# Gated attention in two streams, a softmax divided at the gates, and scan levels 2 and 4 in one group

## The chip, the cores and the metric

The kernel runs on one core of one Trainium2 chip. The metric is the time of one execution on the device in microseconds (us). Before the change it was run three times: 2367.55, 2368.6 and 2372.68 us, a median of 2368.6 us. One more execution was profiled, and all rows of the trace are from that one.

## The reference

Two layers over 2560 tokens (a prompt of 2048 and a sample of 512), 1024 wide. The even layer has two mixers side by side: A, a gated linear attention in both directions (4 heads of 128), and B, softmax attention in a window of 128 tokens to either side (8 query heads of 64 on 2 heads of keys and values). The odd layer is a gated short convolution. Cut to what the change touches:

```python
def swa_mixer(q, k, v, z, rel_bias, sink):
    ...
    s = jnp.einsum('bnqkgd,bnskd->bnkgqs', qh, kb).astype(jnp.float32) + bias
    s = jnp.where(mask, s, -jnp.inf)
    sk = sink.astype(jnp.float32).reshape(SWA_KV_HEADS, SWA_GROUP)[:, :, None, None]
    m = jnp.maximum(jnp.max(s, -1, keepdims=True), sk)
    e = jnp.exp(s - m)
    p = e / (jnp.sum(e, -1, keepdims=True) + jnp.exp(sk - m))
    o = jnp.einsum('bnkgqs,bnskd->bnqkgd', p.astype(v.dtype), vb).reshape(Bn, L, SWA_WIDTH)
    return o * jax.nn.silu(z)
```

In A, token j counts for token i with the weight q_i . (k_j x the product of the decays between them), the decays being numbers below one for each of the 128 channels. `o_f` runs over j <= i and `o_b` over j > i; their sum is normed and multiplied by silu(z).

## The kernel before

The tokens stand in 20 chunks of 128 (`c`) and 5 groups of 512 (`g`; group 4 is the sample, groups 0 to 3 the prompt). The work on TensorE is of two kinds.

*The dense stream* (`dense_ch`, `dense_tok`) are the projections, in a fixed order of stages (`run`, L2103): the input projection of groups 4, 3, 2 and 1, the output projection of group 4, the input projection of group 0, the odd layer of group 4, the output projection of group 0, and so on. A float32 product is made of three fast ones: each operand is split in a high part (`wh`, `st`) and a low one (`wl`). A unit of `dense_ch` (L569) has 16 matmuls of 128x512 on wh and 8 on wl, into one PSUM bank `acc`. ScalarE casts a raw weight tile `ws` to `wh`, GpSimd makes `wl` of the difference in four pieces (`cook`, `cook_low`, L531 to L556). SyncE's queue loads the raw tiles, and every other DMA of the kernel stands in that same queue.

*The side streams* are Python generators, whose pieces are put between the dense matmuls. `gla_stream` (L1454) takes the chunks of a group from the last to the first. For each it runs `inside` (L1186): the decayed products inside a chunk by doubling. At level s (1, 2, 4, ... 64), the queries in the tile Q ("QQ") and the keys in the tile K ("KK") hold the decays inside blocks of s tokens. One level is 16 matmuls of 32x32 (8 of 64x64 at the last), and VectorE grows Q and K to the next level between them. The keys of levels 2 to 16 are copied by ScalarE to a compact tile `km`. At level 8 the queries are copied aside too (`qm`, a tile "md"), and level 8 is computed together with level 16, in one visit to TensorE:

```python
            if s in (8,):
                qm = self.m2(hold=True)
                nc.scalar.copy(qm[:].rearrange("p (b two s) -> p b two s", two=2, s=s), halves(Q, s))
                wait.append((li, s, qm))
```

The same generator then does the chunk's part behind the levels: four transposes of K for each direction, the products with v, the state of the backward direction. Only then does it go on to the next chunk. `along` carries the forward state through the chunks at the end.

`swa_front` (L1510) computes the scores of B, their row maxima (VectorE), exponentials and sums (ScalarE), the reciprocals `den`, and multiplies the four tiles of P by them on VectorE (L1571). `swa_back` (L1579) transposes P on TensorE, splits it in `pth` and `ptl`, multiplies with V, and GpSimd multiplies the result `o` by the gate `gb` for each chunk (L1652).

*The order* is made when the program is built. `Model` (L97) keeps a clock for each engine by a cost for each operation, and when each tile is written and free. `Flow.pump` (L337) runs at each step of the dense stream. It takes the side streams by rank (0, 1, 2), then by the time at which what they wait for is ready, and lets one go on if its time has come and the clocks of VectorE and ScalarE stand less than about 4 us ahead. The scan has rank 1, `swa_front` and `swa_back` rank 2. A stream that says `yield x` waits for a time, for tiles, or for a mark. On the chip each engine runs its own queue in that order and waits on semaphores.

Of the kernel before, what the change touches and what calls it, by code (L numbers as in the profile page):

```python
# [262 lines left out]
class Flow:  # L263
# [32 lines left out]
    def flush(self, everything=False, name=None):  # L296
        now, keep = [], []
        for one in self.late:
            (now if everything or name in one[2] or (name is None and one[0] <= self.t) else keep).append(one)
        self.late = self.model.late = keep  # L300
        for one in now:
            one[1]()
# [74 lines left out]
class Trunk:  # L377
    def __init__(self, tc, nc, I, y_out, ctx):
        self.model = Model()
        self.nc = Engines(nc, self.model)  # L380
        self.tc, self.I, self.y_out = tc, I, y_out
        self.flow = Flow(self.model)
        P = lambda name, bufs, **k: ctx.enter_context(tc.tile_pool(name=name, bufs=bufs, **k))
        self.const = P("const", 1)
        self.stp = P("stp", 8)
        self.wp = P("wp", 2)
        self.yp = P("yp", 4)
        self.e2 = P("e2p", 1)
# [24 lines left out]
        self.bst = None  # L413
        self.blocks = []
# [154 lines left out]
    def dense_ch(self, xh, xl, w=None, last=True):  # L569
# [3 lines left out]
        p = self.pd()  # L573
# [13 lines left out]
        if last:  # L587
            self.drop(wl)
        return p
# [86 lines left out]
    def setup(self):  # L676
# [9 lines left out]
        self.dtot = c.tile([128, NC, 4], F32, name="dtot")  # L686
# [492 lines left out]

    def gla_load_k(self, c):  # L1180
        K = self.e((128, 2, 512), "KK")
        for i in range(2):
            self.nc.sync.dma_start(K[:, i], self.k_s[c])
        return K

    def inside(self, c, first, last, ld, K, ahead):  # L1186
# [3 lines left out]
        Q = self.e((128, 2, 512), "QQ")  # L1190
# [10 lines left out]

        acmp = self.sm((128, 4, 32), "acmp")
# [17 lines left out]
        def grow_k(s):  # L1220
# [12 lines left out]
        Sb = self.bst if not last else None  # L1233
        wait = []
        for li, s in enumerate((1, 2, 4, 8, 16, 32, 64)):
            n = 512 // s
            pls = []
            if s in (8,):
# [3 lines left out]
            else:  # L1242
# [14 lines left out]
                for lt, t, qm in wait:  # L1257
# [3 lines left out]
                    self.drop(qm)  # L1261
# [24 lines left out]
                kms.pop(s, None)  # L1286
# [14 lines left out]
            if s not in (8,):  # L1301
                grow_q()
# [5 lines left out]
            if s in (8,):  # L1308
                grow_q()
# [5 lines left out]
            if s == 4:  # L1315
                v = self.e((128, 512), "v")
                nc.sync.dma_start(v[:], self.v_s[c])
            yield [Q] if s < 16 else [Q, K]
        end = tots[128]
# [3 lines left out]
        nc.vector.tensor_copy(self.dtot[:, c], mk(end, 4, [[1, 4]]))  # L1323
        ahead(0)
        self.flow.defer(lambda: nc.sync.dma_start(self.qf_s[c], Q[:, 1]), Q)

        def turn(i):
# [3 lines left out]
            t = self.e((128, 4, 128), "km", bufs=2)  # L1331
# [3 lines left out]
        def grow(t):  # L1335
            pv = self.pw((128, 4, 128))
            for h in range(4):
                nc.tensor.matmul(pv[:, h], t[:, h], v[:, h * 128:h * 128 + 128], start=True, stop=True)
            return pv

        kf = kb = None
        if not last:
            yield from self.bank()
            kf = turn(0)
# [4 lines left out]
                                  acmp[:].unsqueeze(2).broadcast_to(wide))  # L1349
        if not first:  # L1350
            yield from self.bank()
            kb = turn(1)
        ahead(1)
# [10 lines left out]
        if not first:  # L1364
# [6 lines left out]
            else:  # L1371
                for h in range(4):
                    nc.vector.scalar_tensor_tensor(Sn[:, h], Sb[:, h], mk(end, h, [[1, 1]]), pv[:, h],
# [8 lines left out]
        yield [Q]  # L1382
# [19 lines left out]
    def along(self, c, first, last, ld, ahead):  # L1402
# [13 lines left out]
        if not last:  # L1416
# [4 lines left out]
            else:  # L1421
                for h in range(4):
                    nc.vector.scalar_tensor_tensor(Sn[:, h], Sf[:, h], self.dtot[:, c, h:h + 1], m[:, h],
# [29 lines left out]

    def gla_stream(self):  # L1454
        for g in (4, 3, 2, 1, 0):
# [3 lines left out]
            cs = list(range(4 * g + 3, 4 * g - 1, -1))  # L1459
            ld, K = self.gla_load(cs[0]), self.gla_load_k(cs[0])  # L1460
            nxt = {}
            for i, c in enumerate(cs):
                yield [*ld, K]

                def ahead(n):
                    if i < 3:
                        nxt[n] = (self.gla_load, self.gla_load_k)[n](cs[i + 1])
                yield from self.inside(c, *ends(c), ld, K, ahead)
                ld, K = nxt.get(0), nxt.get(1)
            if 4 * g > c0:  # L1470
                continue
            self.bst = None
            ld = K = None
            nxt.clear()
# [35 lines left out]
    def swa_front(self):  # L1510
# [7 lines left out]
        def best():  # L1518
# [4 lines left out]
            key = (lambda c: c) if "done_e1_0" in done else (lambda c: (-(c // 4), c))  # L1523
# [3 lines left out]
        while left:  # L1527
# [10 lines left out]
            for kv in range(2):  # L1538
# [3 lines left out]
                Pt = self.e((128, 4, 385), "P", bufs=4)  # L1542
# [36 lines left out]
    def swa_back(self):  # L1579
# [17 lines left out]
        for n in range(40):  # L1597
# [20 lines left out]
            for kb in range(nk):  # L1618
# [14 lines left out]
                yield []  # L1633
            yield [pl, V]
            Pt = None
# [15 lines left out]
            yield [gb]  # L1651
# [451 lines left out]
    def run(self):  # L2103
# [70 lines left out]
        flow.add(self.swa_front())  # L2174
        flow.add(self.swa_back())
# [29 lines left out]
```

## Time and profile before

| what | value |
|---|---|
| median of three runs | 2368.6 us (2367.55 to 2372.68) |
| the profiled execution | 2370.12 us |
| its span, first to last instruction | 2368.1 us |
| granted clock of TensorE | 0.998 |
| HBM read and written | 319.72 and 114.84 MB |
| share of the DMA engines by the kernel's own queue | 56.5% |

The span is what the trace shows; 2.0 us of the execution lie around it. An engine's busy time is the union of its instructions. The ends of matmuls are modelled and matmuls overlap each other, so the time that a row of TensorE gives is longer than its share; the step from one row's start to the next row's start is what it costs the queue. A float32 matmul of the scan leaves two records in the trace, a fast or a transposing one leaves one.

### The profile page before, as it was taken

To read this page: it belongs to the slowest core of one execution; us is meant where nothing else is said; L and a number is where in the kernel's file an instruction comes from. 1 tells how busy PE (TensorE), PEld (TensorE's weight loads), DVE (VectorE), ACT (ScalarE), POOL (GpSimd) and SP (SyncE) were. 2 spreads that over 40 slices of the span, in tenths; PEclk is the share of its full clock that TensorE was granted. 3 is DMA by queue.
4 is the path that set the end of the run, shared out by engine and by line. 5 is a ranking of instruction groups with operands and counts; after the bars stand their busy time and mean duration, and the time that the engine had idled before them with its cause. 6 is when DMAs were issued, how large, how long until landed. Compare 5 with 4: busy or idle time off the path is not lost.

```text
span 2368.1 us, 43087 instructions
## 1 busy us (share of the span) xinstructions
PE 2343.9 (99%) x15830; PEld 1951.8 (82%) x15830; DVE 1582.8 (67%) x2699; ACT 1226.1 (52%) x2363; POOL 1418.4 (60%) x1610
## 2 busy tenths in 40 slices
PE   8999999999999999999999999999999999999998
PEld 8888889888988888888888888878888877888887
DVE  2267756767767677577776467876566587656567
ACT  4666776656576645665577532543334343333431
POOL 5454435443444444444444467898887689988674
PEclk9999999999999999999999999999999999999999
DMA  7977686676667657675478777232124633221573
GB/s 230 295 226 233 221 269 229 209 221 221 218 194 236 223 173 242 197 218 161 158 245 268 266 261 243 92 116 89 52 78 140 217 105 103 73 72 58 175 242 121
DMA packets 275057, 437.37 MB, mean 185 GB/s; under 512 B 21360, under 2 KB 160240, under 8 KB 274848
## 3 DMA queue, kind: packets, MB, share of 16 engines
q1 hardware_dynamic: 274848, 434.64, 56.5%
q8 instruction: 125, 2.05, 0.4%
q14 instruction: 84, 0.69, 0.1%
HBM read 319.72 MB, written 114.84 MB: 184 GB/s over the span
## 4 chain that ended last, share of the span: by engine, by line
PE 87%; DVE 5%; POOL 4%; DMA 2%; issue 1%; ACT 1%; SPq 0%; POOLq 0%; DVEq 0%; ACTq 0%
PE acc L242 71%; PE ps L242 17%; POOL wl L242 1%; POOL wh L242 1%; DVE st L242 1%; DVE bst L242 1%; DVE y L242 1%; POOL md L242 0%; SPq L242 0%; DVE QQ L242 0%; DVE P L242 0%; DVE KK L242 0%; DMA K<-kb_s 0%; DMA mix_s<-gb 0%; DMA op_s<-QQ 0%
## 5 line engine op out<-in xcount | busy, mean ns | idle before, releaser
L242 POOL TENSOR_TENSOR wl<-ws,wh 128x256 fp32r<-128x256 f32 (+1 forms) x912 | 750.7, 855 | 711.4 <-PE acc L242 478.0
L242 PE MATMUL acc<-st,wh 128*128 128x512 f32 x3160 | 828.5, 395 | 2.8 <-DVE pr L242 2.0
L242 PEld LDWEIGHTS acc<-st,wh 128*128 128x128 f32 x3160 | 580.9, 188 | 121.0 <-issue 3.1
L242 PE MATMUL acc<-st,wl 128*128 128x512 f32 x1744 | 471.9, 395 | 2.8 <-POOL wl L242 1.9
L242 PE MATMUL acc<-wh,st 128*128 128x512 f32 (+1 forms) x1680 | 389.4, 371 | 7.9 <-ACT st L242 6.4
L242 PEld LDWEIGHTS acc<-st,wl 128*128 128x128 f32 x1744 | 320.8, 188 | 68.0 <-POOL wl L242 4.1
L242 PEld LDWEIGHTS acc<-wh,st 128*128 128x128 f32 x1680 | 300.2, 189 | 55.1 <-ACT st L242 6.4
L242 ACT CAST wh<-ws 128x1024 fp32r<-128x1024 f32 (+2 forms) x252 | 249.0, 989 | 184.2 <-DMA ws<-in_w_oo 55.9
L242 PE MATMUL acc<-wl,st 128*128 128x512 f32 (+1 forms) x840 | 209.0, 368 | 0.6 <-POOL wl L242 0.5
L242 ACT ACTIVATE md<-md 128x512 f32<-128x512 f32 x264 | 164.7, 631 | 20.5 <-DVE md L242 14.9
L242 PEld LDWEIGHTS acc<-wl,st 128*128 128x128 f32 x840 | 150.7, 188 | 23.8 <-POOL wl L242 1.3
L242 DVE SCALAR_TENSOR_TENSOR md<-acc,md 128x512 f32<-128x512 f32 (+1 forms) x113 | 77.0, 683 | 81.5 <-ACT md L242 76.5
L242 DVE TENSOR_TENSOR st<-pr,st 128x512 fp32r<-128x512 f32 x115 | 98.5, 874 | 41.6 <-ACT st L242 41.2
L242 ACT ACTIVATE md<-acc 128x512 f32<-128x512 f32 (+1 forms) x133 | 76.2, 597 | 67.0 <-PE acc L242 66.5
L242 POOL TENSOR_TENSOR wh<-md,wh 128x256 fp32r<-128x256 f32 x118 | 96.7, 842 | 13.6 <-ACT wh L242 13.1
L242 ACT CAST pth<-ps 128x512 fp32r<-128x512 f32 x112 | 65.3, 583 | 73.1 <-PE ps L242 72.3
L242 DVE CUSTOM_DVE_ANT_0 P<-ps,P 128x384 f32<-128x384 f32 (+1 forms) x160 | 79.3, 525 | 29.6 <-PE ps L242 29.0
L242 ACT ACTIVATE P<-P,nm 128x385 f32<-128x385 f32 (+1 forms) x160 | 93.2, 587 | 3.9 <-DVE nm L242 3.9
L242 ACT ACTIVATE mv<-mv,eps 128x1 f32<-128x1 f32 x40 | 11.8, 295 | 151.8 <-DVE mv L242 147.7
L242 PE MATMUL acc<-P,wh 128*128 128x512 f32 x312 | 89.5, 400 | 0.4 <-POOL wh L242 0.4
L242 ACT COPY km<-KK 128x512 f32<-128x512 f32 x80 | 50.8, 635 | 72.2 <-DVE KK L242 50.9
L242 ACT CAST st<-pr 128x512 fp32r<-128x512 f32 x115 | 68.3, 617 | 30.3 <-DMA pr<-mix_s 12.9
(490 smaller groups left out, 4090.2 us busy)
## 6 DMA issues: line engine op xcount, KB each, us to landing
ws<-in_w_ch SPq DMA_DIRECT2D x105, 512.0 KB, 4.4
ws<-in_w_od SPq DMA_DIRECT2D x58, 512.0 KB, 4.2
ws<-in_w_oe SPq DMA_DIRECT2D x40, 512.0 KB, 3.8
ws<-in_w_oo SPq DMA_DIRECT2D x36, 512.0 KB, 3.5
K<-kb_s SPq DMA_DIRECT2D x32, 384.0 KB, 6.3
d_s<-md SPq DMA_DIRECT2D x40, 256.0 KB, 4.2
qb_s<-md SPq DMA_DIRECT2D x80, 128.0 KB, 3.9
tA<-d_s SPq DMA_DIRECT2D x20, 512.0 KB, 5.7
```

The costliest lines, as they stand in the source:

```text
L242: r = f(*a, **k)
```

## The change

It has four parts.

1. *The scan becomes two streams.* What follows the levels moves from `inside` to `behind`, which `gla_behind` runs for each chunk as soon as its levels are done. K, Q and the totals of a chunk are handed over, so the levels of the next chunk can stand beside the rest of the last one. K and Q may now also lie in tiles "y" (`gla_home`), and the transposed K and the copies km in tiles "md". At most two chunks are under way (`self.open`).
2. *Level 2 is done with level 4.* The queries of level 2 are copied aside as those of level 8 are, and the two levels are computed in one visit.
3. *The softmax is divided at the gates.* P is no longer multiplied by the reciprocals. They are stored to `rd_s` as soon as they are there, for both heads of keys, and loaded late, each row spread over 64 partitions, into a tile "md" (`rb`). GpSimd multiplies the gate by them, then the result by the gate.
4. *Ranks and repairs.* `swa_front` and `swa_back` get rank 1, and `swa_front` chooses its chunks by another mark. `dense_ch` holds its bank while it uses it, and `flush` takes a deferred action off its list before it runs it.

```diff
@@ Trunk.__init__
+        self.rd_s = dr("rd_s", (NC, 2, 4, 128))
@@ dense_ch
-        p = self.pd()
+        p = self.pd(hold=True)
...
+        self.drop(p)
@@
+    def gla_home(self, tag):
+        done = self.flow.done
+        rows = "swa_in1" in done and "res_x1_4_3" not in done
+        return [(self.e2, tag, 1)] if rows or self.model.spare(tag, 1) else self.large[:1]
@@ inside
-        Q = self.e((128, 2, 512), "QQ")
+        while self.free_at(self.gla_home("QQ")) > self.flow.t:
+            yield 0.3
+        Q = self.take(self.gla_home("QQ"), (128, 2, 512))
...
+        while self.open > 1:
+            yield 0.3
+        self.open += 1
...
-                    km = kms[2 * s] = self.e((128, 512), "km", bufs=2)
+                    km = kms[2 * s] = self.take([(self.e2, "km", 2)] + self.mids, (128, 512))
...
-            if s in (8,):
+            if s in (2, 8,):
+                while self.free_at(self.mids) > self.flow.t:
+                    yield 0.3
                 qm = self.m2(hold=True)
...
-            if s not in (8,):
+            if s not in (2, 8,):
                 grow_q()
...
-        end = tots[128]
+        nc.vector.tensor_copy(self.dtot[:, c], mk(tots[128], 0, [[1, 8]]))
+        self.heads.append((c, first, last, K, Q, base, acmp))
+        self.flow.mark("head_%d" % c)
+
+    def behind(self, c, first, last, K, Q, base, acmp, v, ahead):
...
-            t = self.e((128, 4, 128), "km", bufs=2)
+            t = self.m2((128, 4, 128), hold=True)
@@
+    def gla_behind(self):
+        nxt = []
+        for c in [*range(19, 15, -1), *range(15, -1, -1)]:
+            yield "head_%d" % c
+            v = nxt.pop() if nxt else self.load_v(c)
...
+            yield from self.behind(*self.heads.pop(0), v, ahead)
@@ swa_front
-                for h in range(4):
-                    nc.vector.tensor_scalar(Pt[:, h, :w], Pt[:, h, :w], den[:, h:h + 1], None, op0=ALU.mult)
-                    if h == 1:
-                        yield []
+                def sums(c=c, kv=kv, den=den):
+                    nc.sync.dma_start(self.rd_s[c, kv].rearrange("h t -> t h"), den[:])
+                    if kv:
+                        self.flow.mark("rd_%d" % c, max(0.0, self.model.clock["sync"] - self.flow.t) + 10.0)
+                self.flow.defer(sums, den)
@@ swa_back
+            if kv:
+                yield "rd_%d" % c
+                while self.free_at(self.mids) > self.flow.t:
+                    yield 0.3
+                rb = self.m2(hold=True)
+                a = self.rd_s
+                for i in range(2):
+                    nc.sync.dma_start(rb[64 * i:64 * i + 64], bass.AP(a.tensor, a.offset + (2 * c + i) * 512, [[0, 64], [1, 512]]))
...
-            yield [gb]
+            yield [gb, rb]
+            flat = gb[:].rearrange("p h t -> p (h t)")
+            nc.gpsimd.tensor_tensor(flat, flat, rb[:], op=ALU.mult)
+            self.drop(rb)
+            yield [o]
             nc.gpsimd.tensor_tensor(gb[:], o[:], gb[:], op=ALU.mult)
@@ run
         flow.add(self.gla_stream(), rank=1)
-        flow.add(self.swa_front())
-        flow.add(self.swa_back())
+        flow.add(self.gla_behind(), rank=1)
+        flow.add(self.swa_front(), rank=1)
+        flow.add(self.swa_back(), rank=1)
```

How the order moves at two places. First TensorE's queue at the first chunk's levels 1 to 4, beside the input projection of group 3 (`acc<-st,wh` and `acc<-st,wl` are dense, `qn,KK` the diagonal, `QQ,KK` level 1, and `QQ,km` levels 2 and 4, each with one visit of its own). Before:

```order
L242 MATMUL acc<-st,wh 128x512 x14
L242 MATMUL ps<-qn,KK 32x32 x16
L242 MATMUL ps<-QQ,KK 32x32 x16
L242 MATMUL acc<-st,wh 128x512 x2
L242 MATMUL acc<-st,wl 128x512 x8
L242 MATMUL acc<-st,wh 128x512 x8
L242 MATMUL ps<-QQ,km 32x32 x16
L242 MATMUL acc<-st,wh 128x512 x8
L242 MATMUL acc<-st,wl 128x512 x8
L242 MATMUL ps<-QQ,km 32x32 x16
L242 MATMUL acc<-st,wh 128x512 x16
```

The same place of the changed kernel, where `md,km` is level 2 with its queries in a copy:

```order
L242 MATMUL ps<-qn,KK 32x32 x16
L242 MATMUL ps<-QQ,KK 32x32 x16
L242 MATMUL acc<-st,wh 128x512 x2
L242 MATMUL acc<-st,wl 128x512 x8
L242 MATMUL acc<-st,wh 128x512 x16
L242 MATMUL acc<-st,wl 128x512 x8
L242 MATMUL acc<-st,wh 128x512 x10
L242 MATMUL ps<-md,km 32x32 x16
L242 MATMUL ps<-QQ,km 32x32 x16
L242 MATMUL acc<-st,wh 128x512 x6
```

Level 2 has moved behind 26 more dense matmuls and stands next to level 4, which has itself moved behind 10 more. In all, TensorE has 13061 matmuls in either program.

Second, GpSimd's queue, where the gates of two chunks stand early in the attention among the low parts of the weights (`wl`). Before:

```order
L242 TENSOR_TENSOR wl<-y,wh 128x168 x4
L242 TENSOR_TENSOR wl<-ws,wh 128x256 x12
L242 TENSOR_TENSOR gb<-gb 128x512
L242 TENSOR_TENSOR wl<-ws,wh 128x256 x20
L242 TENSOR_TENSOR gb<-gb 128x512
```

At the gates of two chunks early in the changed kernel, where `gb<-gb,md` is the multiplication of the gate by the reciprocals:

```order
L242 TENSOR_TENSOR wl<-ws,wh 128x256 x20
L242 TENSOR_TENSOR gb<-gb,md 128x512
L242 TENSOR_TENSOR gb<-gb 128x512
L242 TENSOR_TENSOR wl<-ws,wh 128x256 x32
L242 TENSOR_TENSOR gb<-gb,md 128x512
L242 TENSOR_TENSOR wl<-ws,wh 128x256 x4
L242 TENSOR_TENSOR gb<-gb 128x512
```

A second multiplication has come in front of that of each gate, mostly right before it. On SyncE's queue 40 stores of `den` to `rd_s` and 40 loads of it come in (1304 DMAs before, 1386 after), and VectorE's queue has 160 instructions less.

More of the change, by code (lines that the diff above doesn't have):

```diff
@@ L296, in flush @@
     def flush(self, everything=False, name=None):
[L297 to L300, printed above, removed]
+        now = [one for one in self.late if everything or name in one[2] or (name is None and one[0] <= self.t)]
         for one in now:
-            one[1]()
+            if any(one is x for x in self.late):
+                self.late[:] = [x for x in self.late if x is not one]
+                one[1]()
     def force(self, *tiles):
@@ L1232, in inside @@
         base = None
-        Sb = self.bst if not last else None
         wait = []
@@ L1322, in inside @@
         self.drop(base)
-        nc.vector.tensor_copy(self.dtot[:, c], mk(end, 4, [[1, 4]]))
-        ahead(0)
+        base = None
         self.flow.defer(lambda: nc.sync.dma_start(self.qf_s[c], Q[:, 1]), Q)
@@ L1338, in grow, with place @@
                 nc.tensor.matmul(pv[:, h], t[:, h], v[:, h * 128:h * 128 + 128], start=True, stop=True)
+            self.drop(t)
             return pv
+        def place():
+            yield from self.bank()
+            while self.free_at(self.mids) > self.flow.t:
+                yield 0.3
         kf = kb = None
         if not last:
-            yield from self.bank()
+            yield from place()
             kf = turn(0)
@@ L1349, in inside @@
                                   acmp[:].unsqueeze(2).broadcast_to(wide))
+        self.open -= 1
         if not first:
-            yield from self.bank()
+            yield from place()
             kb = turn(1)
-        ahead(1)
+        self.drop(K)
         yield [A, v] + ([Sb] if Sb is not None else [])
@@ L1452, in seq, with ahead @@
         return (0, 16) if g < 4 else (16, 20)
+    def gla_behind(self):
[3 more added lines that the diff above has]
+            v = nxt.pop() if nxt else self.load_v(c)
+            def ahead():
+                if c not in (0, 16) and "gla_in%d" % ((c - 1) // 4) in self.flow.done:
+                    nxt.append(self.load_v(c - 1))
+            yield from self.behind(*self.heads.pop(0), v, ahead)
+            v = None
     def gla_stream(self):
+        nxt = {}
         for g in (4, 3, 2, 1, 0):
@@ L1458, in gla_stream, with ahead @@
             ends = lambda c: (c == c0, c == c1 - 1)
[L1459 to L1462, printed above, removed]
-                yield [*ld, K]
-                def ahead(n):
-                    if i < 3:
-                        nxt[n] = (self.gla_load, self.gla_load_k)[n](cs[i + 1])
+            for c in range(4 * g + 3, 4 * g - 1, -1):
+                if 0 not in nxt:
+                    nxt[0] = self.gla_load(c)
+                while 1 not in nxt:
+                    if self.free_at(self.gla_home("KK")) <= self.flow.t:
+                        nxt[1] = self.gla_load_k(c)
+                    else:
+                        yield 0.3
+                ld, K = nxt.pop(0), nxt.pop(1)
+                yield [*ld, K]
+                def ahead(s):
+                    if c > c0 and "gla_in%d" % ((c - 1) // 4) in self.flow.done:
+                        if s == 4:
+                            nxt[0] = self.gla_load(c - 1)
+                        elif self.free_at(self.gla_home("KK")) <= self.flow.t:
+                            nxt[1] = self.gla_load_k(c - 1)
                 yield from self.inside(c, *ends(c), ld, K, ahead)
-                ld, K = nxt.get(0), nxt.get(1)
+                ld = K = None
             if 4 * g > c0:
                 continue
+            yield "tail_%d" % c0
             self.bst = None
-            ld = K = None
-            nxt.clear()
             yield "done_e1_%d" % g
```

40 lines of the change are left out of this document (26 added, 14 removed).

## The prediction

> **What bounds the kernel now.** I read the page first: the span, the busy shares, the slices, the chain that ended last.
>
> ```profile
> span 2368.1 us, 43087 instructions
> PE 2343.9 (99%) x15830; PEld 1951.8 (82%) x15830; DVE 1582.8 (67%) x2699; ACT 1226.1 (52%) x2363; POOL 1418.4 (60%) x1610
> PEclk9999999999999999999999999999999999999999
> PE 87%; DVE 5%; POOL 4%; DMA 2%; issue 1%; ACT 1%; SPq 0%; POOLq 0%; DVEq 0%; ACTq 0%
> ```
>
> TensorE is busy for 99% of the span, at the full clock in every slice, and 87% of the chain is its own matmuls. The other engines are free for a third to a half of the time. So the question for every edit is: does it take a matmul, a step between matmuls, or a wait out of TensorE's queue, or put one in? Next I read the engines by stretch, and the waits of TensorE from 100 to 1400 us, where both attentions run beside the dense projections.
>
> ```profile
> 100.00:1250.00 1150.00, 1148.14 (x10441) 966.34 (x10440) 809.03 (x1711) 719.59 (x1474) 513.10 (x643) 1.00 0.68 217
> 1600.00:1800.00 200.00, 200.00 (x875) 163.95 (x874) 119.83 (x149) 75.08 (x108) 171.14 (x179) 1.00 0.23 78
> 1880.00:2368.00 488.00, 475.80 (x2104) 388.55 (x2102) 337.20 (x415) 183.07 (x292) 380.13 (x391) 1.00 0.36 123
> PE ps L242 <- ACT pth L242: 0.7, 1, 0.7
> PE acc L242 <- POOL wl L242: 0.5, 1, 0.5
> PE ps L242 <- DVE acmp L242: 0.2, 1, 0.2
> ```
>
> The columns of a stretch are its length, then busy us and instructions of PE, PEld, DVE, ACT and POOL. In the attention stretch TensorE lacks 1150 - 1148.14 = 1.9 us, and the longest single wait is 0.7 us. So **no wait is there to be won**: at most 1.9 us. The rest of the stretch can only get shorter if TensorE's own stream does. The stretch of 1600 to 1800 us, which has dense matmuls alone, gives the price of one: 200 us / 875 = 0.2286 us.
>
> **The change part by part.** *The matmuls* are the same in number and shape before and after, since the level of 2 is only put off and computed beside the level of 4. What changes is how often TensorE turns from the dense stream to a group of small matmuls and back. The timeline of TensorE at the first chunk shows what a turn costs (start, us, then name, shape and count; a 32x32 matmul of the program leaves two records):
>
> ```profile
> 118.67 3.33 PE L242 MATMUL acc<-st,wh 128*128 128x512 f32 x14
> 121.94 0.46 PE L242 MATMUL ps<-qn,KK 128*32 128x32 f32 x32
> 122.21 0.56 PE L242 MATMUL ps<-QQ,KK 128*32 128x32 f32 x32
> 122.70 0.73 PE L242 MATMUL acc<-st,wh 128*128 128x512 f32 x2
> 123.27 2.00 PE L242 MATMUL acc<-st,wl 128*128 128x512 f32 x8
> 125.10 1.98 PE L242 MATMUL acc<-st,wh 128*128 128x512 f32 x8
> 127.01 0.46 PE L242 MATMUL ps<-QQ,km 128*32 128x32 f32 x32
> 127.40 2.11 PE L242 MATMUL acc<-st,wh 128*128 128x512 f32 x8
> 129.34 1.98 PE L242 MATMUL acc<-st,wl 128*128 128x512 f32 x8
> ```
>
> From 118.67 to 123.27 stand 16 dense matmuls and one visit of two groups (the diagonal and the level of 1): 4.60 us. From 125.10 to 129.34 stand 16 dense matmuls and one visit of one group (the level of 2): 4.24 us. So a second group inside a visit costs 4.60 - 4.24 = 0.36 us, and a visit of its own costs 4.24 - 16 x 0.2286 = 0.58 us. Doing levels 2 and 4 in one visit saves 0.58 - 0.36 = 0.22 us a chunk, and over 20 chunks **4.5 us**. With a dense step between 0.2275 and 0.2295 the same sum gives 4.8 and 4.2 us. These microseconds lie on TensorE's queue with nothing beside them, so they come off the end.
>
> *Neighbours.* The two attentions are also given the same rank and the scan two streams, and the planner's order has fewer turns altogether: counted over the whole order of TensorE, the stretches of short matmuls between dense ones are 460 before and 394 after. Twenty of the 66 are the merged levels. In the other 46 two pieces that had a visit each now stand side by side. Three places show what that is worth:
>
> ```profile
> 293.81 1.98 PE L242 MATMUL acc<-st,wl 128*128 128x512 f32 x8
> 296.11 0.60 PE L242 MATMUL ps<-ident,P 128*128 128x128 f32 x4
> 296.46 0.71 PE L242 MATMUL acc<-st,wh 128*128 128x512 f32 x2
> 297.01 0.27 PE L242 MATMUL ps<-ident,KK 128*128 128x128 f32 x1
> ...
> 818.14 1.08 PE L242 MATMUL ps<-wh,st 128*128 128x512 f32 x4
> 819.40 1.18 PE L242 MATMUL ps<-wh,st 128*128 128x512 f32 x4
> 820.42 1.08 PE L242 MATMUL acc<-wh,st 128*128 128x512 f32 x4
> ...
> 824.98 1.08 PE L242 MATMUL ps<-wh,st 128*128 128x512 f32 x4
> 826.37 0.63 PE L242 MATMUL ps<-wl,st 128*128 128x512 f32 x2
> 826.84 0.40 PE L242 MATMUL ps<-wh,st 128*128 128x512 f32 x1
> ```
>
> Four transposes alone (between 818.14 and 820.42, with 8 dense matmuls) cost 2.28 - 1.83 = 0.45 us. Two value matmuls alone (from 824.98 to 826.84, with 6) cost 1.86 - 1.37 = 0.49. Both in one visit (from 293.81 to 297.01, with 10) cost 3.20 - 2.29 = 0.91. Standing together saves 0.03 us at best, and perhaps nothing. I take 0.02 for each of the 46, **0.9 us**, between 0 and 1.4.
>
> *The softmax division.* The 160 multiplications of P by the reciprocals leave VectorE, two small stores and two loads a chunk come to the SyncE queue, and one multiplication a chunk comes to GpSimd. The rows, with least, median and greatest ns of one, then GpSimd's wait and the ScalarE copy:
>
> ```profile
> L242 DVE TENSOR_SCALAR P<-P,den x160: 343/417/962, 162.3 to 1233.3; 128x384 f32<-128x384 f32 x128, 128x256 f32<-128x256 f32 x32
> L242 POOL TENSOR_TENSOR gb<-gb x20: 1280/1292/1801, 233.0 to 1259.8; 128x512 f32<-128x512 f32 x20
> POOL wl L242 <- PE acc L242: 434.8, 110, 10.3
> L242 ACT COPY md<-QQ 128x512 f32<-128x512 f32 x20 | 12.4, 619 | 0.0
> ```
>
> VectorE loses at least 160 x 0.417 = 67 us of work. It is busy for 809 of 1150 us there and TensorE waits 0.2 us at a time for it, so this is worth **nothing by itself**. GpSimd gains 20 x 1.29 = 26 us, most of them right behind the gate's multiplication, so that wl stands behind 2.6 us where it stood behind 1.3. From 100 to 1400 us GpSimd sat for 434.8 us, 110 times, waiting for TensorE to give back a wl buffer: a lead of 434.8 / 110 = 4.0 us each time. That hides 1.3 us more. Without that lead each would cost up to 1.3 us, 26 in all. ScalarE gains 20 copies of level 2's queries at 0.62 us, 12 us, under an engine busy for 720 of 1150 us. Tiles K, Q and km that now find room in other pools, and P tiles held longer, move DMAs and no arithmetic. I count them at nothing, and the ends of that are in the second rival.
>
> *The round trip of the reciprocals.* The store writes 128 x 4 pieces of four bytes, which no row of this trace shows. The load of a chunk stands in the same SyncE queue, and the code puts it at least 10 us behind the store. SyncE works in order: if the store lands later than that, everything behind the load waits too, the weights (ws) first, then ScalarE's wh, then wl and TensorE. The nearest rows are the one load in pieces of four bytes, 128 of them, and the slowest of the transfers that come often:
>
> ```profile
> L242 SPq DMA_DIRECT2D norm_g<-in_norm_g x1: 327/327/327, 8.8 to 8.8; - x1
> DMA to landing us min/median/max: 3.7/3.7/3.7
> K<-kb_s SPq DMA_DIRECT2D x32, 384.0 KB, 6.3
> ```
>
> I take 3.7 to 6.3 us: covered, nothing. If time went with the pieces, four times as many would take 4 x 3.7 = 14.8 us. That end is kept for the first rival.
>
> *The sum.* 4.5 + 0.9 = 5.4 us less. The profiled execution took 2370.1 us, 2.0 more than its span, and would take 2364.7. The median of the runs shown, 2368.6, is 1.5 below the profiled one, so the time is **2363.2 us**, 0.23% less.
>
> **The rivals.** *First: the round trip holds SyncE (slower).* Place: the 20 loads of the reciprocals. The cover is the 10 us in the code and GpSimd's lead of 4.0 us, 14.0 together. At a landing of 14.8 us each chunk loses 0.8 us, 16 in all: 2379 us. The change is slower by over 0.2% once 5.4 + 4.7 = 10.1 us are lost, 0.5 us a chunk, from a landing of 14.5 us on. For it: a store in pieces of four bytes is new here, and the queue is in order. Against it: the row of 128 such pieces took 3.7 us, less than the 6.3 of 384 KB. The Trainium skill speaks for this rival: its page "DMA: Bandwidth & Descriptors", section "Specifications", says that pieces below 512 bytes make the engine read, modify and write. The same page, in "Latency and other measured facts", gives 0.2 us for an access to HBM on average and 2 us at high load. If each of an engine's 32 pieces (512 over 16 engines) read and wrote one after another, an estimate by that page is 12.8 us on average, still covered, and 128 us at high load, which would add some 2,300 us. No run here shows such a store; norm_g's pieces were a load.
>
> *Second: bunching (no difference).* The order after has the short matmuls closer together. Counted in pieces (four transposes, two value matmuls, one level), 100 dense matmuls carried at most 29 before, and carry 36 and 37 now at the two fullest places. VectorE and ScalarE must empty the banks of both there, and a dense group whose bank is not free stops TensorE. The price of a tight stretch is in the row of 1880 to 2368 us: 488 - 475.8 = 12.2 us, 2.5%. On the two places, some 40 us each (100 x 0.2286 + 37 x 0.45), that is 2.0 us: 2365.2 us. If it spread to a sixth of the stretch, 4.8 us: 2368. Over all 1150 us it would be 28.8: 2392. Against it: VectorE has 67 us less to do, and the waits now are 1.9 us in all.
>
> *Third: the merged visit saves less (no difference).* The 0.36 us for a second group is from one place, where both groups read KK. Levels 2 and 4 read two copies (km), and the first of them a copy of the queries too. If their second group cost 0.43, a chunk saves 0.15, the sum is 3.0 + 0.9 = 3.9 us, and the time 2364.7. For it: one place is little. Against it: what a visit costs beyond its matmuls is the turn from the dense stream and back, and that is made once less in any case.
>
> **How the numbers follow.** The measurement can tell 0.2%, 4.7 us, from no change, and my 5.4 stands hardly beyond it. The forecast, a gain of 4.7 to 8.1 us (at best the waits go too: 4.8 + 1.4 + 1.9), has 0.53: 2360.5 to 2363.9. Bunching that costs 1 to 10 us, with 0.24, and the smaller gain, with 0.08, end within 0.2%: 0.32, up to 2373. The first rival has 0.06, bunching over a third of the stretch and more has 0.09. So faster 0.53, same 0.32, slower 0.15. The range goes 1.5 us below the best case for the spread of the runs (2367.55 to 2372.68), to 2359, and up to 2376, which leaves out about 0.03 below and 0.10 above.
>
> **What would show it.** *Right:* in TensorE's timeline, the visits of levels 2 and 4 become one a chunk, which costs near 0.94 us (4.60 - 16 x 0.2286); TensorE's waits from 100 to 1250 us stay under 3 us; GpSimd's wait for TensorE stays over 350 us; rd_s lands in 4 to 7 us. *Wrong:* waits of TensorE behind ACT, DVE or wl that sum to more than 5 us there, or SyncE waiting for rd_s, or visits of two groups that cost 1.1 us.

## The result and the profile after

The changed kernel takes 2492.2 us (median of 4 runs, 2490.78 to 2501.03) where the kernel before takes 2369.36 (2367.55 to 2372.68): a ratio of 1.0523, with a 95% interval of 1.0508 to 1.0538. It is 122.8 us slower, far outside the predicted range of 2359 to 2376 us. First the page of the changed kernel: its span, the busy shares, the clock in 40 slices, and the kernel's own DMA queue (packets, MB, share of the 16 engines' time).

```profile
span 2490.1 us, 43136 instructions
PE 2376.1 (95%) x15830; PEld 1977.9 (79%) x15830; DVE 1507.9 (61%) x2539; ACT 1236.4 (50%) x2385; POOL 1440.8 (58%) x1630
PEclk9999998999999999999999999999999999999999
q1 hardware_dynamic: 299456, 439.97, 62.3%
```

TensorE is busy for 95% instead of 99%, and no other engine's share has risen (61, 50 and 58% after 67, 52 and 60). Only the DMA queue is fuller, 62.3% of a longer span, 56.5% before, with 5.33 MB more (439.97 against 434.64). So the span is lost by waiting, and the next view is the stretches (the first as before; the second so long that TensorE has done as many records in it; columns as in the prediction, then the granted clock, the share of the DMA engines and GB/s).

```profile
100.00:1250.00 1150.00, 1064.93 (x9849) 895.57 (x9848) 677.10 (x1415) 654.52 (x1300) 479.44 (x596) 0.97 0.78 201
100.00:1370.00 1270.00, 1177.70 (x10429) 989.78 (x10428) 739.54 (x1559) 730.92 (x1520) 529.17 (x658) 0.97 0.79 202
```

The work that TensorE did in 1150 us before (10441 records) now takes some 1270 (10429). In these 1270 us it is idle for 1270 - 1177.7 = 92.3 us, where 1.9 were idle before: 90 us more. Its busy time for the same work is 1177.7 - 1148.1 = 29.6 us longer, and the granted clock is 0.97 instead of 1.00. Together that is 120 of the 123 us, so the whole loss lies here. What TensorE waited for in these 1270 us, then waits of GpSimd and of SyncE's queue in the whole span (us in total, times, longest):

```profile
PE ps L242 <- DVE QQ L242: 14.1, 8, 4.4
PE ps L242 <- DMA QQ<-qf_s: 9.5, 3, 5.2
PE acc L242 <- ACT wh L242: 6.8, 2, 6.4
PE ps L242 <- DMA KK<-k_s: 6.5, 1, 6.5
PE ps L242 <- DVE y L242: 5.8, 4, 3.8
PE ps L242 <- ACT A L242: 5.6, 2, 5.3
...
POOL wl L242 <- PE acc L242: 358.9, 101, 17.7
POOL gb L242 <- DMA md<-rd_s: 64.7, 10, 13.0
...
SPq L242 <- DMA rd_s<-den: 41.7, 18, 5.5
```

No single producer stands out. The longest of these waits are 4 to 6.5 us, on loads that the change does not touch (qf_s, k_s) or on engines that may have waited for a load themselves. A profile in which many things are late by some microseconds suggests something that all share. SyncE's queue does wait for rd_s, 41.7 us in 18 waits, which is the first rival's mechanism. The experiments had to tell whether that is the cause.

### The profile page after: what moved, and what is told of

It reads as the page before. It is cut to its first block, busy times and chain, and to the rows that moved or that the text cites. A ratio compares the mean times of both kernels' runs of the same rounds, so it can differ in the third digit from the quotient of the medians.

```text
span 2490.1 us, 43136 instructions
## 1 busy us (share of the span) xinstructions
PE 2376.1 (95%) x15830; PEld 1977.9 (79%) x15830; DVE 1507.9 (61%) x2539; ACT 1236.4 (50%) x2385; POOL 1440.8 (58%) x1630
## 3 DMA queue, kind: packets, MB, share of 16 engines
q1 hardware_dynamic: 299456, 439.97, 62.3%
## 5 line engine op out<-in xcount | busy, mean ns | idle before, releaser
L242 PE MATMUL acc<-st,wh 128*128 128x512 f32 x3080 | 803.7, 396 | 2.7 <-POOL wh L242 1.4
L242 PEld LDWEIGHTS acc<-st,wh 128*128 128x128 f32 x3080 | 572.3, 189 | 119.6 <-POOL wh L242 2.3
L242 PE MATMUL acc<-st,wl 128*128 128x512 f32 x1704 | 459.3, 397 | 2.1 <-POOL wl L242 1.2
L242 DVE TENSOR_TENSOR ptl<-ps,pth 128x512 fp32r<-128x512 f32 x112 | 75.9, 681 | 27.0 <-ACT pth L242 26.8
L242 ACT CAST wh<-md 128x512 fp32r<-128x512 f32 x59 | 36.4, 619 | 100.2 <-DVE md L242 42.3
```

Of the source, the lines that this page charges most:

```text
L242: r = f(*a, **k)
```

## The experiments

Ratios are against runs of the kernel before on the same chip (21 to 29 of them, with medians of 2368.53 to 2368.85 us), with their 95% interval.

### Which part: all but part 3

`e1_no_part3` is the changed kernel with P divided on VectorE again.

```diff
-                def sums(c=c, kv=kv, den=den):
-                    nc.sync.dma_start(self.rd_s[c, kv].rearrange("h t -> t h"), den[:])
...
+                for h in range(4):
+                    nc.vector.tensor_scalar(Pt[:, h, :w], Pt[:, h, :w], den[:, h:h + 1], None, op0=ALU.mult)
...
-            nc.gpsimd.tensor_tensor(flat, flat, rb[:], op=ALU.mult)
```

> The changed kernel with part 3 alone undone: P is multiplied by the reciprocals on VectorE again, and there is no rd_s, no store, no load, and no second multiplication on GpSimd. Parts 1, 2 and 4 stay. Store theory (the stores in pieces of four bytes hold up the DMA engines, and the weights behind them): the 123 us go and the rest of the prediction comes through, 2364 us (2358 to 2369). Load theory (the loads that read one 2 KB line 64 times do it): the same. Order theory (two streams of equal rank bunch the short matmuls, and TensorE waits for VectorE and ScalarE): the order stays bunched, so most of the loss stays, 2450 us or more.

Measured: 2369.68 us, 1.0002 (0.9993 to 1.0011). Two streams, merged levels and new ranks together are no difference; the loss is in part 3. The gain that was expected with it, 2364 us, does not come either.

### Which half of part 3: the store, or the load

`e2_store_only` is the kernel before (P still divided on VectorE), and den is stored beside it as in the change, to be read by nobody.

```diff
+        self.rd_s = dr("rd_s", (NC, 2, 4, 128))
...
+                def sums(c=c, kv=kv, den=den):
+                    nc.sync.dma_start(self.rd_s[c, kv].rearrange("h t -> t h"), den[:])
+                self.flow.defer(sums, den)
```

> The kernel before, with only the 40 stores of the reciprocals added, 128 x 4 pieces of four bytes into one line of 2 KB each; nothing reads them. Store theory: 40 stores of some 3 us each, 2460 to 2495 us. Load theory and order theory: no change, 2367 to 2373 us.

Measured: 2503.23 us, 1.056 (1.0533 to 1.0587). Forty stores of 2 KB cost 134 us, 3.4 us each, with no load anywhere that could wait for them. That is more than the 2495 us expected at most, and it rules out the load in SyncE's queue as the cause.

`e3_load_only` is the kernel before with the 40 loads, each reading one line of 2 KB for 64 partitions, and the gate's multiplication put behind their arrival. `e11_load_lines` has the same order and reads another line for each partition.

```diff
+                for i in range(2):
+                    nc.sync.dma_start(rb[64 * i:64 * i + 64], bass.AP(a.tensor, a.offset + (c + i) % 8 * 512, [[0, 64], [1, 512]]))
...
-            yield [gb]
+            yield [gb, rb]
```

```diff
-                    nc.sync.dma_start(rb[64 * i:64 * i + 64], bass.AP(a.tensor, a.offset + (c + i) % 8 * 512, [[0, 64], [1, 512]]))
+                    nc.sync.dma_start(rb[64 * i:64 * i + 64], a[128 * c + 64 * i:128 * c + 64 * i + 64, :512])
```

> The kernel before, with only the 40 loads added: 2 KB of a line that was written long ago, read 64 times each into the half of a tile md; GpSimd does not use them, though its gate multiplication is put behind their arrival. Load theory: 2430 us or more. Store theory and order theory: no change, 2367 to 2374 us.

> As the run with the loads alone, in the same order of all engines, but each of the 64 partitions reads a line of its own (a row of x) and not all the same 2 KB. Same-line theory: the 30 us go, 2367 to 2374 us. If the volume, the places in the SyncE queue or the wait of GpSimd cost the 30 us: 2395 to 2402 us.

Measured: 2399.08 us, 1.0124 (1.0108 to 1.0141), and 2398.44 us, 1.0127 (1.0113 to 1.0141). One line read 64 times costs what 64 lines cost. But the kernel before does lose 30 us by such loads, which no theory of the first run had; where they go comes below, with the merged levels, since it is the same place.

### What it is in the store

`e6_store_spread` has the same instructions in the same order on every engine as `e2_store_only`, and the same 512 pieces of four bytes in each store. Only the addresses differ: each piece lies in a line of 512 bytes of its own. `e12_store_64` gives each 64 bytes. `e2b_store_16B` writes the same 2 KB by token: 128 pieces of 16 bytes, neighbours still side by side.

```diff
-        self.rd_s = dr("rd_s", (NC, 2, 4, 128))
+        self.rd_s = dr("rd_s", (NC, 2, 4, 128, 128))
...
-                    nc.sync.dma_start(self.rd_s[c, kv].rearrange("h t -> t h"), den[:])
+                    nc.sync.dma_start(self.rd_s[c, kv][:, :, 0].rearrange("h t -> t h"), den[:])
```

```diff
+        self.rd_s = dr("rd_s", (NC, 2, 4, 128, 16))
```

```diff
+        self.rd_s = dr("rd_s", (NC, 2, 128, 4))
...
+                    nc.sync.dma_start(self.rd_s[c, kv], den[:])
```

> As the run with the stores alone, in the same order of all engines, but each piece of four bytes goes to a line of 512 bytes of its own in HBM. If the number of small pieces is what costs, the time is that of the stores alone, 2460 us or more. If it is that all 16 DMA engines write into the same lines at the same time, most of the loss goes: 2369 to 2390 us. Load theory and order theory: 2367 to 2373 us.

> The kernel before with the stores alone, each four-byte piece in 64 bytes of its own in place of 512. Same-line theory with lines of 64 bytes or less: no change, 2367 to 2373 us. If pieces within 512 bytes of each other still collide (8 pieces share 512 bytes here, 128 in the run that lost 134 us): 2380 to 2480 us.

> The kernel before with the stores alone, but laid out as they lie in SBUF: 128 pieces of 16 bytes, one for each token, in the same 2 KB. A fourth of the pieces, as close together. If each piece that meets others in its line costs: 134 / 4 = 34 us, 2395 to 2410 us. If only the number of bytes of a line under writing counts: as before, 2490 us or more. If 16 bytes in one piece are enough: 2367 to 2373 us.

Measured: 2368.91 us, 0.9999 (0.999 to 1.0008); 2368.32 us, 0.9992 (0.998 to 1.0004); 2367.9 us, 1.0003 (0.9994 to 1.0012). All three are free. So it is neither the number of pieces, nor their four bytes by themselves, nor the 2 KB: it is **pieces of four bytes packed side by side**. The pages of `e2_store_only` and `e6_store_spread` (span, then the DMA queue) show on what the price falls, for the same packets and bytes:

```profile
span 2506.7 us, 43175 instructions
q1 hardware_dynamic: 295968, 434.72, 61.1%
```

```profile
span 2366.6 us, 43175 instructions
q1 hardware_dynamic: 295968, 434.72, 57.0%
```

Each DMA engine is busy for 0.611 x 2506.7 = 1531.6 us in the one and 0.570 x 2366.6 = 1349.0 in the other. The difference of 182.6 us is 4.6 us for each store on each of the 16 engines, and the kernel loses 3.4 of them.

This busy time is hardly that of the stores' own pieces. The two traces record every packet of every DMA (a packet is one piece that an engine moves): all four-byte packets together account for 2.3 of the 182.6 us, with a median of 9 ns in both. Nearly all the rest stands on other transfers. No packet in `e6_store_spread` takes over 2.2 us; in `e2_store_only` 453 take over 2.4, up to 9.6, and 450 of these have 512 bytes or more. All 450 start 1.0 to 11.0 us behind the first four-byte packets of a store. So the pieces leave fast, and what comes behind them stands still. The ten us from 164 on, behind the first store, show it (`e2_store_only`, then `e6_store_spread`; columns as above):

```profile
164.00:174.00 10.00, 8.82 (x84) 8.20 (x82) 0.54 (x4) 3.86 (x6) 4.14 (x8) 1.00 0.72 47
```

```profile
164.00:174.00 10.00, 10.00 (x122) 9.49 (x122) 4.13 (x9) 4.52 (x8) 4.14 (x8) 1.00 0.67 203
```

The engines are about equally busy, 0.72 and 0.67, but move 47 GB/s in the one and 203 in the other. For comparison, a load of 512 KB of weights, in the page of the kernel before (count, KB, median us from issue to landing):

```profile
ws<-in_w_ch SPq DMA_DIRECT2D x105, 512.0 KB, 4.4
```

A store of 2 KB thus costs every engine about as much time as such a load takes to land, and the transfers behind it are late. The timeline of `e2_store_only` behind one store (start, us; in brackets the idle time before and who ended it):

```profile
162.71 0.37 SPq L242 DMA_DIRECT2D rd_s<-den  x1
...
166.48 0.45 SPq L242 DMA_DIRECT2D pr<-in_xT  x1
...
176.12 1.23 DVE L242 TENSOR_TENSOR QQ<-qn,tA 128x1024 f32<-128x1024 f32 x1 [11.58 <-DMA pr<-in_w_tok]
...
177.40 0.57 PE L242 MATMUL ps<-QQ,KK 128*32 128x32 f32 x32 [4.58 <-DVE QQ L242]
...
178.29 0.62 ACT L242 CAST st<-pr 128x512 fp32r<-128x512 f32 x1 [8.99 <-DMA pr<-in_xT]
```

The same store, load and consumers in `e6_store_spread`:

```profile
162.29 0.37 SPq L242 DMA_DIRECT2D rd_s<-den  x1
...
165.77 0.48 SPq L242 DMA_DIRECT2D pr<-in_xT  x1
...
170.81 0.62 ACT L242 CAST st<-pr 128x512 fp32r<-128x512 f32 x1 [1.93 <-DMA pr<-in_xT]
...
172.22 0.56 PE L242 MATMUL ps<-QQ,KK 128*32 128x32 f32 x32
```

ScalarE uses the load of pr 5.0 us after its issue with the spread store, and 11.8 us after it with the packed one. VectorE waits 11.58 us for a DMA before it grows QQ, and so TensorE stops for 4.58 us at the group of level 1; in the other kernel it doesn't stop there.

### The same test in the changed kernel

`e14_after_spread` is the changed kernel with the same order on every engine and the store spread to 512 bytes. In `e5_rows` den is transposed on TensorE first, and the store is four rows of 512 bytes.

```diff
-                    nc.sync.dma_start(self.rd_s[c, kv].rearrange("h t -> t h"), den[:])
+                    nc.sync.dma_start(self.rd_s[c, kv, :, :, 0].rearrange("h t -> t h"), den[:])
...
-                a = self.rd_s
+                a = self.I["x"]
```

```diff
+                nc.tensor.transpose(pr[:4], den[:], self.ident[:])
...
+                nc.scalar.copy(dt[:4, :128], pr[:4])
...
-                    nc.sync.dma_start(self.rd_s[c, kv].rearrange("h t -> t h"), den[:])
+                    nc.sync.dma_start(self.rd_s[c, kv], dt[:4, :128])
```

> The changed kernel in the same order on every engine: only the store's addresses differ (each four-byte piece in a line of 512 bytes of its own), and the loads read a row of x in place of the reciprocals, so that the output of the window attention is scaled by other numbers. Same-line theory: the 123 us go, 2366 to 2374 us. If the number of small pieces, the added loads, the second multiplication on GpSimd or the order of the changed kernel cost a part, that part stays: more than 2385 us.

> The changed kernel, with the reciprocals of a chunk and key head transposed on TensorE and copied by ScalarE to 4 rows, so that the store has 4 pieces of 512 bytes instead of 512 pieces of 4. The loads stay. Same-line theory (many small writes into one line are what holds the DMA engines up): the stores' loss goes and the loads' 30 us stay, 2390 to 2405 us. If the loads cost nothing beside the stores: 2372 us (2369.7 and 40 visits of one transpose, near 0.1 us each). If any store to rd_s that is read again costs: 2450 us or more.

Measured: 2375.95 us, 1.0029 (1.0018 to 1.0041), and 2375.35 us, 1.0024 (1.0015 to 1.0033). The difference of `e14_after_spread` to the changed kernel is 2492.2 - 2375.95 = 116.3 us, from nothing but the addresses of the store (the load reads other lines as well; `e11_load_lines` showed no price for which lines are read). As it reads x, this load no longer waits for the store. In `e5_rows` it does, and the time is the same, with no wait of SyncE for rd_s in its trace: the round trip by itself costs nothing that can be seen. Neither time was expected quite so: `e14_after_spread` ends 2 us above its range, and in `e5_rows` the 30 us of the loads, expected to stay, are not there. The stores themselves show where the 116 us went: least, median and greatest ns of an issue, then the start of the first and the last, in the changed kernel and in `e14_after_spread`.

```profile
L242 SPq DMA_DIRECT2D rd_s<-den x40: 359/378/1552, 159.3 to 1370.8; - x40
```

```profile
L242 SPq DMA_DIRECT2D rd_s<-den x40: 359/378/1327, 160.6 to 1254.1; - x40
```

From the first store to the last it is 1211.5 us in the one and 1093.5 in the other: the 118 us are lost between the stores, and none behind them. What is left of part 3 without that price, the loads, the gate's second multiplication and the order around them, is 2375.95 - 2369.68 = 6.3 us above `e1_no_part3`.

### The other parts: streams, merged levels, ranks

`e8_streams_only` is `e1_no_part3` without the merged levels, `e7_merge_only` the kernel before with the merged levels alone, `e13_rank2` is `e1_no_part3` with the softmax attention at its old rank.

```diff
-            if s in (2, 8,):
+            if s in (8,):
```

```diff
-            if s in (8,):
+            if s in (2, 8,):
                 qm = self.m2(hold=True)
```

```diff
-        flow.add(self.swa_front(), rank=1)
-        flow.add(self.swa_back(), rank=1)
+        flow.add(self.swa_front())
+        flow.add(self.swa_back())
```

> The changed kernel with parts 2 and 3 undone: the two streams, the tiles in other pools, the ranks and the repairs alone. If the waits that ate the gain come from the streams: 2369.7 + 4.5 = 2374 us (2372 to 2376). If they come from the merged level, and the streams cost nothing: 2368 us (2367 to 2370).

> The kernel before with part 2 alone: the queries of level 2 are copied aside and levels 2 and 4 are done in one visit. By the prediction's sum 20 x 0.22 = 4.5 us less: 2364.4 us (2363.8 to 2365.0). If the new order costs waits of TensorE as it did with the other parts (6.6 us of idle TensorE from 100 to 1250 us against 1.9): 2368 to 2371 us.

> Parts 1 and 2 (the run without part 3), with the window attention at rank 2 as it was before, to see whether the equal rank is what bunches the work and eats the gain of the merged level. If so TensorE's idle time from 100 to 1250 us falls from 6.6 to about 2 us and the time is 2365 us (2363 to 2367). If the waits come from the two streams and the merged level themselves: 2368 to 2371 us.

Measured: 2370.31 us, 1.0009 (1.0001 to 1.0018); 2406.86 us, 1.0158 (1.0144 to 1.0172); 2371.67 us, 1.0012 (1.0003 to 1.0021). The merged visit in TensorE's timeline of `e1_no_part3`, at the first chunk:

```profile
131.43 2.43 PE L242 MATMUL acc<-st,wh 128*128 128x512 f32 x10
133.78 0.46 PE L242 MATMUL ps<-md,km 128*32 128x32 f32 x32
134.06 0.49 PE L242 MATMUL ps<-QQ,km 128*32 128x32 f32 x32
134.48 1.65 PE L242 MATMUL acc<-st,wh 128*128 128x512 f32 x6
135.97 1.98 PE L242 MATMUL acc<-st,wl 128*128 128x512 f32 x8
```

From 131.43 to 135.97 stand 16 dense matmuls and one visit of two groups: 4.54 - 16 x 0.2286 = 0.88 us for the visit, where 0.94 was predicted and two visits of one group cost 2 x 0.58 = 1.16. The changed kernel takes the same 4.54 us there (130.18 to 134.72). So at this place the merged visit saves what it should. The stretch of 100 to 1250 us shows what became of it, in `e8_streams_only`, `e1_no_part3`, `e13_rank2` and `e14_after_spread`:

```profile
100.00:1250.00 1150.00, 1148.27 (x10443) 967.88 (x10442) 803.93 (x1709) 719.20 (x1473) 514.58 (x643) 1.00 0.68 218
```

```profile
100.00:1250.00 1150.00, 1143.38 (x10435) 969.01 (x10434) 811.74 (x1707) 727.87 (x1496) 514.56 (x644) 1.00 0.68 218
```

```profile
100.00:1250.00 1150.00, 1139.02 (x10420) 963.59 (x10419) 815.33 (x1707) 728.31 (x1504) 519.04 (x639) 1.00 0.68 218
```

```profile
100.00:1250.00 1150.00, 1137.54 (x10410) 963.50 (x10409) 743.22 (x1551) 728.38 (x1504) 533.70 (x656) 1.00 0.71 223
```

TensorE is idle there for 1.7 us with the streams alone, 6.6 with the merged levels, 11.0 with the old rank and 12.5 with part 3 and a spread store. The merged levels bring 4.9 us of waits, as much as the 4.5 us they save, and `e1_no_part3` is 0.6 us below `e8_streams_only`, less than can be told apart. The equal rank is not what makes the waits: with the old one there are more.

`e7_merge_only` loses 38 us, which neither of its expectations had, in another place. Its stretch from 1250 to 1560 us, then the same of `e3_load_only` and of the kernel before:

```profile
1250.00:1560.00 310.00, 279.86 (x1298) 229.27 (x1299) 199.91 (x297) 148.93 (x396) 166.06 (x179) 0.92 0.72 240
```

```profile
1250.00:1560.00 310.00, 290.56 (x1359) 239.68 (x1359) 206.72 (x300) 147.62 (x373) 184.05 (x199) 0.96 0.70 236
```

```profile
1250.00:1560.00 310.00, 306.54 (x1430) 252.86 (x1429) 212.12 (x289) 146.67 (x335) 205.72 (x220) 0.99 0.65 219
```

TensorE does 132 records fewer than before in `e7_merge_only`, 132 x 0.2286 = 30 us of the 38, and 71 fewer in `e3_load_only`. The attentions end late: the last store of a mixed result (mix_s) starts at 1435.2 us in `e7_merge_only`, 1414.8 in `e3_load_only`, 1358.4 before. The dense stage behind needs all of them, and dense work to put beside their end runs short. In `e1_no_part3`, which has the merged levels beside parts 1 and 4, that store starts at 1359.0: something in parts 1 and 4 makes the merged levels affordable. It is not the rank, since `e13_rank2` has the old one and takes 2371.67 us; the second stream is the likeliest, but no run has it without the tiles in other pools and the repairs. Why loads alone stretch the single stream so much was not tried further; it is argued from these rows that holding tiles longer delays the next pieces.

## Why the prediction was wrong

**What bounds the kernel**: right. TensorE was idle for only 1.9 us in the attention stretch, so what it waits for late loads adds to the time: 90 us of waits and 29.6 us at a lower clock are nearly all of the loss.

**The round trip of the reciprocals** is the step that failed: "I take 3.7 to 6.3 us: covered, nothing". It took the store for a transfer with a landing time, and asked only who waits for this transfer. Nobody has to: in `e2_store_only` nothing reads it, and it costs 134 us. The term was worth 116 us here, because a store of packed pieces holds up whatever follows it on the 16 engines that carry everybody's loads: 4.6 us on each, by the pair of runs above. The nearest row, norm_g's 128 pieces of four bytes landing in 3.7 us, was a load, and bounded neither the direction nor the neighbourhood of the pieces. Even the landing was not the point: spread, the same 512 pieces land in about the predicted time (`e6_store_spread`, least, median and greatest):

```profile
DMA to landing us min/median/max: 1.9/3.4/7.6
```

**The first rival** had the right culprit and the right sign, at a chance of 0.06, but the wrong mechanism and price: loads of rd_s holding SyncE's queue, 16 us. That wait exists (41.7 us in 18 times) and is a consequence: it is gone in `e5_rows`, whose load still follows its store. The rule that stood with it, from the Trainium skill, page "DMA: Bandwidth & Descriptors", section "Specifications", says that pieces below 512 bytes make the engine read, modify and write. By that rule every store of four-byte pieces should pay, and the runs differ: 512 such pieces a store at a spacing of 512 or of 64 bytes cost nothing (0.9999 and 0.9992). The measurement decides: size alone had no price here, size with neighbours had. That packed pieces are read and written in the same line in turn would fit both, and is argued, not shown.

**The merged levels**, 4.5 us: right as a saving of TensorE's own stream (0.88 us a visit, at one place), given back as waits of 4.9 us. **Neighbours**, 0.9 us: not seen; with the streams alone the kernel is 0.09% above that before, which lies within the 0.2% that can be told. **The second rival**, bunching, had the right sign beneath the loss: in `e14_after_spread` the idle time is 12.5 - 1.9 = 10.6 us, more than the whole forecast of 5.4, and the time 7.4 us above the kernel before. The waits of that run behind VectorE, ScalarE and wl from 100 to 1250 us sum to 10.8 us, above the 5 that were named as a sign of being wrong. That the denser order makes them was not tested; part 3's loads and second multiplication are in them too.

**The softmax division** off VectorE, nothing by itself: right. VectorE's work in the stretch falls from 809.03 to 743.22 us in `e14_after_spread`, 66 us where 67 were predicted, and no time comes of it. GpSimd's lead shrank more than the prediction allowed for: from 100 to 1400 us, the stretch in which it waited 434.8 us for TensorE before, the wait is 248.9 us in the changed kernel and 323.2 in `e14_after_spread`, below the 350 named. The second multiplication is not the only reason, since `e1_no_part3` without it has 342.0. The rows of the changed kernel and of `e14_after_spread`, then what TensorE waits for wl in the latter from 100 to 1250 us:

```profile
POOL wl L242 <- PE acc L242: 248.9, 50, 17.7
```

```profile
POOL wl L242 <- PE acc L242: 323.2, 74, 10.9
PE acc L242 <- POOL wl L242: 2.6, 3, 1.8
```

So "covered" came out nearly right: at most 2.6 us, where 0.5 were before, and `e5_rows` has no wait of TensorE for wl there. Of the four signs of being right, only the visit held. TensorE's waits under 3 us did not, in the changed kernel or in any with two streams and merged levels, and GpSimd's wait did not. The landing of rd_s has no row in the changed kernel; in `e14_after_spread` its median is 3.8 us, just under the 4 to 7 named.

## What to carry to other kernels

A store that scatters single elements is priced by what it does to the transfers behind it, not by its bytes or its landing time: here pieces of 16 bytes, or 64 bytes of room for each, or a transpose on TensorE first took that price away, so try these, and compare the busy share of the DMA queue at equal packets. When all waits grow a little and no producer stands out, look for a shared resource that is fuller, and test it by changing as little as the addresses while every queue keeps its order. Fewer turns on a full engine are worth nothing if what feeds it comes in bunches: count the idle time beside the saving.

## What the runs showed of the hardware that was not expected

- A store of 512 pieces of four bytes, side by side in 2 KB, adds 4.6 us of busy time to each of the 16 DMA engines. Its own packets take 9 ns at the median; packets of other transfers that start 1 to 11 us behind it stand still, up to 9.6 us. The same pieces 64 or 512 bytes apart, or the same 2 KB in pieces of 16 bytes, cost no time. Where between 4 and 16 bytes, and between 4 and 64 bytes of spacing, the limit lies, and whether it is in the engines or in the memory, stays open.
- Idle gaps cost twice. In the changed kernel the granted clock over 1270 us is 0.97, and equal work is 29.6 us longer beside the 90 us of gaps. The Trainium skill, page "TensorE: Matmul & The Clock Gate", section "What's actually happening", gives an idle window of about 3.4 us for the fall to half rate. The trace agrees on the half rate: its clock record has 17 stretches at 0.5 in these 1270 us, 3.4 or 6.8 us long and 78.5 us in all. It does not need a wait of that length. Ten of the 17 come with a gap of TensorE of 3.5 to 6.5 us, seven with gaps of at most 1.5 to 3.1 us, and the measurement decides. `e14_after_spread` has one such stretch, behind a wait of 2.0 us that ends at 766.26 us (its longest wait from 100 to 1250 us, then the clock behind it):

```profile
PE ps L242 <- DVE QQ L242: 2.2, 2, 2.0
768.00:770.00 2.00, 2.00 (x37) 1.50 (x37) 1.96 (x8) 0.42 (x2) 0.00 (x0) 0.50 0.79 238
```

- One line of 2 KB read by 64 partitions costs no more than 64 lines: 2399.08 and 2398.44 us.
